# A hybrid encoder trunk on one core: the memory values' store moves eight pieces down SyncE's queue, the first w_in loads go ahead of the last memory products, and x's strips start in the memory stage's first half

## The chip, the cores and the metric

The kernel runs on one core of a Trainium2 chip. The metric is the device time of one execution in microseconds. It was run three times: 928.7, 930.54 and 930.84 us, median 930.54 us. A further execution was recorded by the hardware profiler and took 931.73 us; the profile and the trace are of that one.

## The reference

Two layers of one mixer. In each, the normed input is projected by one large matrix `w_in`, whose columns feed three groups of heads (a gated convolution, differential attention, and cross-attention into 256 memory tokens), and the three results are projected back by `w_out` and added to x. The memory side needs only `mem`, `mem_norm_g` and `w_mem_kv`:

```python
for l in range(DEPTH):                        # DEPTH = 2
    h = rmsnorm(x, norm_g[l])
    proj = h @ w_in[l]                        # (256, 2048) @ (2048, 7168)
    ...
    mn = rmsnorm(mem, mem_norm_g[l])
    mkv = mn @ w_mem_kv[l]                    # (256, 2048) @ (2048, 1024)
    mk = rmsnorm(mkv[..., :W_MEM].reshape(b, N_MEM, MEM_HEADS, MEM_HEAD_DIM), mem_k_norm_g[l])
    mv = mkv[..., W_MEM:].reshape(b, N_MEM, MEM_HEADS, MEM_HEAD_DIM)
    mq = rmsnorm(m_q.reshape(b, s, MEM_HEADS, MEM_HEAD_DIM), mem_q_norm_g[l])
    y_m = memory_attention(mq, mk, mv).reshape(b, s, W_MEM) * jax.nn.silu(m_g)

    y = jnp.concatenate([y_a, y_d, y_m], axis=-1) @ w_out[l]
    x = x + y
```

All inputs are float32. x and mem are 256 rows of 2048.

## The kernel before

**The products.** Every float32 operand is split into a rounded part `hi` and a remainder `lo`, and a product is three TensorE matmuls: hi by hi, hi by lo, lo by hi (`products`, L295 to L304). The stationary operand is a 128 by 128 piece of the turned activations (`memT` for the memory tokens, `xT` for x, `yT` for the mixer's results); the moving one is a 128 by 512 piece of a weight.

**Pieces of weights.** Weights stream through SBUF in pieces of 512 KB. A piece is loaded by SyncE's queue (SP in the profile) into one of four `raw` buffers; ScalarE (ACT) writes its `hi`, VectorE (DVE) its `lo`, into one of four buffers each; then TensorE uses it in twelve matmuls. A raw buffer is free for the next load when DVE has made `lo`, and a hi buffer when TensorE is done with the piece four places earlier.

**The memory stage.** The keys and values of the memory tokens are made for both layers at the start (L816 to L903). This document counts its pieces 0 to 31, sixteen for each layer: piece s is rows 128·k to 128·k + 127 of `w_mem_kv[l]`, with l, k = divmod(s, 16). `Memory.load` issues a load (L756, or L749 for a piece of w_in), `Memory.make` writes hi and lo (L773 and L774, or L766 for a piece of w_in), `Memory.times` the products. Two halves are accumulated beside each other, keys (half 0) and values (half 1), each in two PSUM banks of four. Pieces 14 and 15, 16 and 17, and 30 and 31 are taken in groups of two: within a group first the keys of both pieces, then the values. When the last keys of a layer are done, `keep_keys` copies them out of PSUM (ACT, L872, tile `kraw`); when the values are done, `keep_values` writes them to `mv` (ACT, L877), and for the second layer stores them to DRAM (SP, L880, tile `mvd`), from where they are loaded back in the second layer (L909).

**The first pieces of w_in.** After piece 31 come the eight pieces of w_in's first block, which are loaded, made and kept ready by the same class; this document calls them w0 to w7. w0 and w1 multiply the first quarter of `xT`, w2 and w3 the second, and so on. From then on `block` and `load_w` (L288 to L292) stream the rest of w_in and w_out in the same way.

**x's strips.** `xT` is made in four quarters q. `strips_by_rows` (L630 to L637) fetches a quarter of x by eight DMAs of 64 KB from GpSimd's queue (POOL) into an `xt` tile, of which there are two; for q = 0 a copy on POOL (L634) reads one value of a given tile first, which holds the DMAs back until that tile is written. After a number of pieces DVE turns the tile (L642, tile `xf`), and ACT and DVE write its hi and lo parts to `xT` (L261, L262). The tile of q = 2 is that of q = 0 again, and is free once DVE has turned it; so with q = 3 and q = 1. Behind the strips POOL's queue carries the DMAs that turn the memory keys (L724, L725).

**What sets the order.** Engines work off their queues in order. Calls wrapped in `pin` or `keep_in_program_order` keep their written order; the others are placed by a scheduler when the program is built. `beside(s)` hangs side work on piece s; `tasks` are generators that `run_side` resumes after a number of pieces (`later(g, n)`: n pieces from now). `m.load(ahead)` at L901 asks for loads up to four pieces ahead, after the products of a group are written.

Of the kernel before, what the change touches and what calls it, by code (L numbers as in the profile page):

```python
# [10 lines left out]
F32 = mybir.dt.float32  # L11
# [7 lines left out]
P = 128  # L19
D_MODEL = 2048  # L20
SEQ = 256
DEPTH = 2
NT = SEQ // P
KT = D_MODEL // P
W_MEM = 512
# [7 lines left out]
NB = 512  # L33
# [14 lines left out]
def encoder(ctx: ExitStack, tc: tile.TileContext, x, mem, norm_g, w_in, conv_w, conv_b,  # L48
            dq_g, dk_g, lq1, lk1, lq2, lk2, head_g, mem_norm_g, w_mem_kv, mq_g, mk_g, w_out, out):
    nc = tc.nc  # L50
    x, mem, out = x[0], mem[0], out[0]

    def pool(name, bufs, space=None):
        kw = {"space": space} if space is not None else {}
        return ctx.enter_context(tc.tile_pool(name=name, bufs=bufs, **kw))
# [7 lines left out]
    dram = pool("dram", 1, bass.MemoryType.DRAM)  # L63
# [6 lines left out]
    def nm(s):  # L70
        uid[0] += 1
        return f"{s}_{uid[0]}"
# [59 lines left out]
    def g_norm(l, k):  # L132
        return gx[:, l * KT + k:l * KT + k + 1]
# [56 lines left out]
    def rsqrt(t, n, vec=None):  # L190

        vec = vec or nc.vector
        y = small.tile([P, n], F32, tag=f"rs_y{n}", name=nm("rsy"))
        a = small.tile([P, n], F32, tag=f"rs_a{n}", name=nm("rsa"))
        yi = y.bitcast(I32)
        vec.tensor_scalar(yi, t.bitcast(I32), 1, None, ALU.logical_shift_right)
        vec.tensor_scalar(yi, yi, -1.0, float(0x5F3759DF), ALU.mult, ALU.add)
        for _ in range(3):
            vec.scalar_tensor_tensor(a, y, -0.5, y, ALU.mult, ALU.mult)
            vec.tensor_tensor(a, a, t, ALU.mult)  # L200
            vec.scalar_tensor_tensor(y, a, 1.5, y, ALU.add, ALU.mult)
        return y
# [4 lines left out]
    side, tasks = deque(), []  # L207
# [3 lines left out]
    def later(g, n):  # L211
        due[id(g)] = chunk[0] + n
        return g
# [40 lines left out]
    def split_T(dst, k, src, gain, pin=False):  # L254

        hi, lo = dst[:, 0, k, :], dst[:, 1, k, :]
        if gain is None:
            both = (nc.scalar.copy(hi, src),  # L258
                    nc.vector.tensor_tensor(lo, src, hi.bitcast(F32), ALU.subtract))
        else:  # L260
            both = (nc.scalar.activation(hi, src, AF.Copy, scale=gain),  # L261
                    nc.vector.scalar_tensor_tensor(lo, src, gain, hi.bitcast(F32), ALU.mult, ALU.subtract))  # L262
        if pin:
            for i in both:
                tc.keep_in_program_order(i)
        made.add((id(dst), k))
# [81 lines left out]
    R, HR, R2_64, R2_128, HR2, R2 = range(6)  # L348

    def col(st, which, t):  # L350
        return st[:, which, t:t + 1]
# [261 lines left out]
    def rows_T(src, k, n):  # L613

        pt = ps_t.tile([P, 2, SEQ], F32, tag="t", name=nm("pt"))
        for j in range(n):
            for t in range(NT):
                tc.keep_in_program_order(
                    nc.tensor.transpose(pt[:, j, t * P:(t + 1) * P], src(k + j, t), ident))  # L619
        return [pt[:, j, :] for j in range(n)]  # L620

    def strips_of(src):

        st = tmp.tile([P, SEQ // B, B * QT], F32, tag="e", name=nm("xt"))
        for b in range(NA):
            tc.keep_in_program_order(nc.sync.dma_start(
                st[b * B:(b + 1) * B], src[:, b * B * QT:(b + 1) * B * QT].rearrange("(n p) r -> p n r", p=B)))
        return st

    def strips_by_rows(src, after=None):  # L630

        st = tmp.tile([P, SEQ // B, B * QT], F32, tag="e", name=nm("xt"))
        if after is not None:
            tc.keep_in_program_order(nc.gpsimd.tensor_copy(st[:, 0, 0:1], after))  # L634
        for n in range(SEQ // B):
            tc.keep_in_program_order(nc.gpsimd.dma_start(  # L636
                st[:, n], src[n * B:(n + 1) * B].rearrange("p (b r) -> b p r", b=NA)))  # L637
        return st

    def turn_strips(st):  # L640
        whole = tmp.tile([P, QT, SEQ], F32, tag="sh", name=nm("xf"))
        tc.keep_in_program_order(nc.vector.transpose(whole.rearrange("p j (n i) -> p j n i", i=B),  # L642
                                                     st.rearrange("p n (c j) -> p j n c", j=QT)))
        return whole

    def x_turned(dst, l, q, src, after=None, wait=2):

        st = strips_of(src) if l else strips_by_rows(src, after)
        yield wait
        whole = turn_strips(st)  # L650
        yield
        for j in range(QT):
            split_T(dst, q * QT + j, whole[:, j], g_norm(l, q * QT + j), pin=True)
            if j % 2:
                yield
# [13 lines left out]
    def T_tile(what):  # L669
        kept.append(big.tile([P, 2, KT, SEQ], F32R, tag="T", name=nm(what)))  # L670
        return kept[-1]
# [11 lines left out]
    memT = T_tile("memT")  # L683
    ssm = const.tile([P, NT, 4], F32, name="ssm")

    pin = tc.keep_in_program_order

    def mem_tokens(lo, n):
        return pin(nc.sync.dma_start(xs[:, :, lo:lo + n], mem[:, lo:lo + n].rearrange("(t p) c -> p t c", p=P)))  # L689
# [4 lines left out]
    def mem_squares(c):  # L694

        for t in range(NT):
            sq = tmp.tile([P, NB], F32, tag="nat", name=nm("msq"), bufs=3)
            pin(nc.scalar.activation(sq, xs[:, t, c * NB:(c + 1) * NB], AF.Square, accum_out=ssm[:, t, c:c + 1]))

    def mem_stats():  # L700

        vec = Steps()
        t = small.tile([P, NT], F32, tag="ssum", name=nm("ssum"))
        y = stm[0]
        vec.tensor_reduce(t, ssm, AX.X, ALU.add)
        vec.tensor_scalar(t, t, 1.0 / D_MODEL, EPS, ALU.mult, ALU.add)
        r = rsqrt(t, NT, vec=vec)
        vec.tensor_copy(y[:, R], r)
        vec.scalar_tensor_tensor(y[:, R2_128], r, 1.0 / P, r, ALU.mult, ALU.mult)
        yield from vec.run(6)  # L710
# [97 lines left out]
    mkT, mv, stm, away = [], [], [], []  # L808
    m = Memory()
    xT = T_tile("xT")  # L810
# [24 lines left out]
    m.begin(1, 1, 0)  # L835
    m.begin(1, 0, 1)

    def beside(s):

        l, k = divmod(s, KT)  # L840
        if l == 0:
            if k % 2 and 3 <= k < KT - 1:
                m.split(k + 1, rows_T(mem_columns, k + 1, 2))
            if k in (3, 6):
                mem_tokens({3: 2, 6: 3}[k] * NB, NB)
            if k in (3, 5, 8, 11):
                mem_squares((3, 5, 8, 11).index(k))
            if k in (8, 10, 12):
                x_natural((k - 8) // 2)
            if k in (6, 7, 8):  # L850
                load_constants(k - 6)
            if k == 9:
                load_norm()
            if k == 11:
                tasks.append(later(mem_stats(), 1))
        else:
            if k == 0:
                x_natural(3)
            if k in (4, 5, 7, 8):
                for t in range(NT):  # L860
                    x_square((4, 5, 7, 8).index(k), t, pin=True)
            if k == 10:
                rest_of_constants()
            if k in (2, 3, 6, 9):
                q = k // 3
                tasks.append(later(x_turned(xT, 0, q, x[:, q * NB:(q + 1) * NB], stm[0][:, R, 0:1] if q == 0 else None,
                                            (3, 5, 5, 5)[q]), 0))

    def keep_keys(l):
        kraw = keep.tile([P, NT, NB], F32, tag="ga", name=nm("kraw"))  # L870
# [4 lines left out]
    def keep_values(l):  # L875
        for t in range(NT):
            pin(nc.scalar.activation(mv[l][:, t, :], m.acc[l, 1][t], AF.Copy, scale=col(stm[0], R, t)))  # L877
        if l > 0:
            away.append(dram.tile([P, NT, W_MEM], F32, name=nm("mvd")))
            nc.sync.dma_start(away[-1], mv[l])  # L880

    s = 1
    while s < DEPTH * KT:
        l, k = divmod(s, KT)
        group = (s, s + 1) if k in (KT - 2, 0) else (s,)
        for i in group:
            beside(i)
        for i in range(s, min(group[-1] + (2 if s == 1 else 3), DEPTH * KT + 1)):
            m.make(i)
        for half in range(2):  # L890
            for i in group:
                m.times(i, half)
            if s == 1 and half == 0:
                m.split(2, rows_T(mem_columns, 2, 2))
            if k == KT - 2:
                (keep_keys, keep_values)[half](l)
                if l + 1 == DEPTH and half == 0:
                    m.make(DEPTH * KT + 1)
        for i in group:
            for ahead in range(i + 1, i + 5):  # L900
                m.load(ahead)  # L901
            run_side(1)
        s = group[-1] + 1  # L903

    for l in range(DEPTH):
# [142 lines left out]
        if l + 1 < DEPTH:  # L1048
            xT = T_tile("xT")
# [50 lines left out]
```

## Time and profile before

| | us |
|---|---|
| median of three runs | 930.54 |
| the profiled execution's own time | 931.73 |
| its span, first to last instruction | 930.0 |
| TensorE busy in the span | 920.0 |
| VectorE busy | 668.6 |
| ScalarE busy | 495.2 |
| GpSimd busy | 37.7 |
| DMA engines, mean of what they moved | 231 GB/s |

Times in rows of the profile are counted from the first instruction. A row of the timeline gives start, length, engine, line and operation, with how many alike follow each other (x2), and in brackets how long the engine was idle before it and what ended that. A matmul's row shows its whole pipeline time of about 0.39 us; the next one starts 0.23 us after it. `PEclk` is the share of TensorE's clock that was granted.

### The profile page before, as it was taken

How to read it: one execution, taken by the hardware profiler on the slowest of the kernel's cores; microseconds unless marked ns; L12 is line 12 of the kernel's file. 1: busy time of each engine (PE TensorE's matmuls, PEld its weight loads, DVE VectorE, ACT ScalarE, POOL GpSimd, SP SyncE). 2: the span in 40 equal slices, each digit the busy share in tenths (PEclk: the TensorE clock that was granted, in tenths of full speed). 3: DMA queues.
4: the chain of work that ended last, by engine and by line, in shares of the span. 5: the costliest groups of instructions: out<-in, count | busy, mean ns of one | idle time of the engine just before them, and what ended most of it. 6: DMA issues, size and time to landing. Idle time of an engine off the chain costs nothing.

```text
span 930.0 us, 12261 instructions
## 1 busy us (share of the span) xinstructions
PE 920.0 (99%) x4168; PEld 762.2 (82%) x4168; DVE 668.6 (72%) x1176; ACT 495.2 (53%) x751; POOL 37.7 (4%) x66
## 2 busy tenths in 40 slices
PE   8999899999999999999999999999999999999998
PEld 6888688888888888888888888888888888888886
DVE  5579867857799787467667757887898777558652
ACT  5666645576465554445455544568554554446431
POOL 2155010000000000000000000000000000000000
PEclk9999899999999999999999999999999999999999
DMA  8889778885669999988587756886889889978662
GB/s 280 277 237 246 251 249 241 236 240 182 183 205 227 270 248 248 242 257 255 199 270 253 243 185 222 236 240 184 237 235 218 259 213 258 248 238 239 212 217 76
DMA packets 247022, 215.10 MB, mean 231 GB/s; under 512 B 132130, under 2 KB 172912, under 8 KB 246960
## 3 DMA queue, kind: packets, MB, share of 16 engines
q1 hardware_dynamic: 242080, 208.71, 76.6%
q0 software_dynamic: 3680, 4.56, 2.2%
q10 hardware_dynamic: 1200, 1.07, 0.4%
q8 instruction: 32, 0.52, 0.2%
q14 instruction: 30, 0.25, 0.1%
HBM read 193.26 MB, written 20.97 MB: 230 GB/s over the span
## 4 chain that ended last, share of the span: by engine, by line
PE 97%; DMA 1%; ACT 1%; SPq 0%; DVE 0%; issue 0%; DVEq 0%
PE acc L302 93%; PE po L442 2%; DMA raw<-in_w_mem_kv_dram 1%; PE s L595 1%; PE s L550 1%; PE s L549 1%; DMA raw<-in_w_in_dram 1%; PE pt L619 0%; ACT hi L766 0%; SPq L754 0%; SPq L689 0%; DVE lo L774 0%; ACT mv L877 0%; ACT hi L773 0%; ACT kraw L872 0%; ACT sq L359 0%
## 5 line engine op out<-in xcount | busy, mean ns | idle before, releaser
L302 PE MATMUL acc<-hi,xT 128*128 128x512 f32 x1792 | 563.8, 393 | 3.0 <-ACT hi L766 3.0
L291 ACT CAST hi<-raw 128x1024 fp32r<-128x1024 f32 x280 | 294.1, 1051 | 340.9 <-PE acc L302 286.5
L292 DVE TENSOR_TENSOR lo<-raw,hi 128x1024 fp32r<-128x1024 f32 x280 | 342.0, 1223 | 185.5 <-ACT hi L291 180.8
L302 PEld LDWEIGHTS acc<-hi,xT 128*128 128x128 f32 x1792 | 337.8, 189 | 72.7 <-ACT hi L766 3.4
L302 PE MATMUL acc<-lo,xT 128*128 128x512 f32 x896 | 350.4, 391 | 0.0
L302 PEld LDWEIGHTS acc<-lo,xT 128*128 128x128 f32 x896 | 169.0, 189 | 34.7 <-DVE lo L766 0.8
L302 PE MATMUL acc<-hi,yT 128*128 128x512 f32 x512 | 158.1, 389 | 0.0
L302 PEld LDWEIGHTS acc<-hi,yT 128*128 128x128 f32 x512 | 96.1, 188 | 20.1
L302 PE MATMUL acc<-lo,yT 128*128 128x512 f32 x256 | 99.7, 389 | 0.0
L302 PE MATMUL acc<-hi,memT 128*128 128x512 f32 x248 | 77.2, 395 | 0.4 <-ACT memT L258 0.4
L302 PEld LDWEIGHTS acc<-lo,yT 128*128 128x128 f32 x256 | 48.1, 188 | 9.8
L302 PEld LDWEIGHTS acc<-hi,memT 128*128 128x128 f32 x248 | 46.0, 188 | 10.4 <-ACT memT L258 0.8
L774 DVE SCALAR_TENSOR_TENSOR lo<-raw,cva,hi 128x1024 fp32r<-128x1024 f32 (+1 forms) x34 | 41.0, 1220 | 17.6 <-ACT hi L773 17.4
L302 PE MATMUL acc<-lo,memT 128*128 128x512 f32 x124 | 46.5, 392 | 0.8 <-DVE lo L774 0.8
L773 ACT ACTIVATE hi<-raw,cva 128x1024 fp32r<-128x1024 f32 (+1 forms) x34 | 36.5, 1096 | 13.6 <-DMA raw<-in_w_mem_kv_dram 6.7
L302 PEld LDWEIGHTS acc<-lo,memT 128*128 128x128 f32 x124 | 23.3, 188 | 6.3 <-DVE lo L774 1.5
L560 ACT ACTIVATE e<-e,mx 128x256 f32<-128x256 f32 x48 | 23.8, 498 | 1.4 <-DVE mx L556 1.4
L636 POOL DMA_DIRECT2D xt<-in_x_dram x32 | 21.5, 678 | 12.8 <-DMA xt<-in_x_dram 6.6
L261 ACT ACTIVATE xT<-xf,gx 128x256 fp32r<-128x256 f32 x32 | 14.3, 499 | 6.0 <-DVE xf L642 5.9
L404 DVE STREAM_TRANSPOSE sh<-sh 128x1024 f32<-128x1024 f32 (+2 forms) x14 | 17.3, 1237 | 0.0
L554 DVE SCALAR_TENSOR_TENSOR e<-dist,s 128x512 f32<-128x512 f32 x24 | 15.7, 680 | 2.2 <-PE s L550 1.7
L1061 DVE TENSOR_TENSOR xs<-acc,xs 128x256 f32<-128x256 f32 (+1 forms) x24 | 10.9, 504 | 7.8 <-PE acc L302 7.8
(161 smaller groups left out, 578.7 us busy)
## 6 DMA issues: line engine op xcount, KB each, us to landing
raw<-in_w_in_dram SPq DMA_DIRECT2D x192, 512.0 KB, 4.5
raw<-in_w_out_dram SPq DMA_DIRECT2D x64, 512.0 KB, 4.4
raw<-in_w_in_dram SPq DMA_DIRECT2D x64, 256.0 KB, 4.0
raw<-in_w_mem_kv_dram SPq DMA_DIRECT2D x30, 512.0 KB, 7.0
d<-sh SPq DMA_DIRECT2D x80, 128.0 KB, 3.9
sh<-d SPq DMA_DIRECT2D x64, 128.0 KB, 4.4
d<-yn SPq DMA_DIRECT2D x40, 64.0 KB, 4.0
yn<-d SPq DMA_DIRECT2D x40, 64.0 KB, 3.7
```

The costliest lines, as they stand in the source:

```text
L261: both = (nc.scalar.activation(hi, src, AF.Copy, scale=gain), nc.vector.scalar_tensor_tensor(lo, src, gain, hi.bitcast(F32), ALU.mult, ALU ...
L291: nc.scalar.copy(hi, raw)
L292: nc.vector.tensor_tensor(lo_, raw, hi.bitcast(F32), ALU.subtract)
L302: i = nc.tensor.matmul(acc, left, right, start=start, stop=stop)
L404: tc.keep_in_program_order(nc.vector.transpose(src, src))
L442: nc.tensor.matmul(po[:, t, :], eT[:, i, t, k, :], v[:, k, h * P:(h + 1) * P], start=k == 0, stop=k == NT - 1)
L554: nc.vector.scalar_tensor_tensor(e[:, c], dist, -slopes[h], s[c], ALU.mult, ALU.add)
L560: nc.scalar.activation(e[:, c, i], e[:, c, i], AF.Exp, bias=mx[:, c, i:i + 1], accum_out=sm[:, c, i:i + 1])
L636: tc.keep_in_program_order(nc.gpsimd.dma_start(st[:, n], src[n * B:(n + 1) * B].rearrange("p (b r) -> b p r", b=NA)))
L773: both = (nc.scalar.activation(hi[:, j], raw[:, j], AF.Copy, scale=g), nc.vector.scalar_tensor_tensor(lo[:, j], raw[:, j], g, hi[:, j].bit ...
L774: nc.vector.scalar_tensor_tensor(lo[:, j], raw[:, j], g, hi[:, j].bitcast(F32), ALU.mult, ALU.subtract))
L1061: nc.vector.tensor_tensor(xc, acc[t][:, lo:lo + n], xc, ALU.add)
```

## The change

Three edits, all in the memory stage. The store of the second layer's values becomes a task that is issued eight pieces later, pinned to its place in SP's queue. For the last group (pieces 30 and 31) the loads of the pieces up to w3 are asked for before the group's products rather than after them. x's strips are asked for at pieces 13 and 15 of the first half and 3 and 6 of the second, rather than at 2, 3, 6 and 9 of the second; the first quarter's copy on POOL now reads column 13 of `memT` in place of the norm's `stm`; and the number of pieces between fetching and turning becomes 5, 7, 7 and 8 rather than 3, 5, 5 and 5.

```diff
@@ -835,6 +835,9 @@
+    def x_strips(q, after, wait):
+        tasks.append(later(x_turned(xT, 0, q, x[:, q * NB:(q + 1) * NB], after, wait), 0))
+
     def beside(s):
...
@@ -853,6 +856,8 @@
             if k == 11:
                 tasks.append(later(mem_stats(), 1))
+            if k in (13, 15):
+                x_strips(k // 14, memT[:, 0, 13, 0:1].bitcast(F32) if k == 13 else None, 2 * (k // 14) + 5)
         else:
...
@@ -861,10 +866,8 @@
             if k == 10:
                 rest_of_constants()
-            if k in (2, 3, 6, 9):
-                q = k // 3
-                tasks.append(later(x_turned(xT, 0, q, x[:, q * NB:(q + 1) * NB], stm[0][:, R, 0:1] if q == 0 else None,
-                                            (3, 5, 5, 5)[q]), 0))
+            if k in (3, 6):
+                x_strips(k // 3 + 1, None, k // 3 + 6)
...
@@ -876,8 +879,12 @@
         if l > 0:
-            away.append(dram.tile([P, NT, W_MEM], F32, name=nm("mvd")))
-            nc.sync.dma_start(away[-1], mv[l])
+            tasks.append(later(put_away(mv[l]), 8))
+
+    def put_away(values):
+        away.append(dram.tile([P, NT, W_MEM], F32, name=nm("mvd")))
+        pin(nc.sync.dma_start(away[-1], values))
+        yield
...
@@ -887,6 +894,9 @@
         for i in range(s, min(group[-1] + (2 if s == 1 else 3), DEPTH * KT + 1)):
             m.make(i)
+        if group[-1] == DEPTH * KT - 1:
+            for ahead in range(s + 2, s + 6):
+                m.load(ahead)
         for half in range(2):
...
@@ -897,8 +907,9 @@
         for i in group:
-            for ahead in range(i + 1, i + 5):
-                m.load(ahead)
+            if group[-1] < DEPTH * KT - 1:
+                for ahead in range(i + 1, i + 5):
+                    m.load(ahead)
             run_side(1)
```

What this does to the queues is shown at three places, in the order in which the built programs hold the instructions.

SP's queue where the memory stage ends; `raw` rows at L756 are pieces of w_mem_kv, at L749 pieces w0 to w7 of w_in, `mvd` is the store of the values. Before:

```order
L756 DMA raw_894<-in_w_mem_kv_dram 128x1024
L756 DMA raw_916<-in_w_mem_kv_dram 128x1024
L749 DMA raw_942<-in_w_in_dram 128x2x512
L749 DMA raw_964<-in_w_in_dram 128x2x512
L880 DMA mvd_1007<-mv_113 128x1024
L749 DMA raw_1009<-in_w_in_dram 128x2x512
L749 DMA raw_1013<-in_w_in_dram 128x2x512
L749 DMA raw_1131<-in_w_in_dram 128x2x512
L749 DMA raw_1153<-in_w_in_dram 128x2x512
```

And now:

```order
L756 DMA raw_898<-in_w_mem_kv_dram 128x1024
L756 DMA raw_918<-in_w_mem_kv_dram 128x1024
L749 DMA raw_946<-in_w_in_dram 128x2x512
L749 DMA raw_968<-in_w_in_dram 128x2x512
L749 DMA raw_974<-in_w_in_dram 128x2x512
L749 DMA raw_976<-in_w_in_dram 128x2x512
L749 DMA raw_1129<-in_w_in_dram 128x2x512
L749 DMA raw_1151<-in_w_in_dram 128x2x512
L886 DMA mvd_1169<-mv_113 128x1024
```

The store stood between w1 and w2; it now stands behind w5.

POOL's queue at the strips of x, a copy and eight DMAs of 64 KB for each of the four quarters, and the first DMAs for the keys (`kd`). Before:

```order
L114 DMA gx<-in_norm_g_dram 128x8x4
L634 COPY xt_660<-stm 128x1
L636 DMA xt_660<-in_x_dram 128x1x128 x8
L636 DMA xt_691<-in_x_dram 128x1x128 x8
L636 DMA xt_772<-in_x_dram 128x1x128 x8
L636 DMA xt_853<-in_x_dram 128x1x128 x8
L724 DMA kd_918<-sh_588 32x4x256 x4
```

And now:

```order
L114 DMA gx<-in_norm_g_dram 128x8x4
L634 COPY xt_540<-memT_107 128x1
L636 DMA xt_540<-in_x_dram 128x1x128 x8
L636 DMA xt_589<-in_x_dram 128x1x128 x8
L636 DMA xt_706<-in_x_dram 128x1x128 x8
L636 DMA xt_791<-in_x_dram 128x1x128 x8
L724 DMA kd_920<-sh_607 32x4x256 x4
```

The queue's order is the same; what its first copy waits for is another tile.

ACT's queue at the border between the two layers, pieces 15 to 18 (L773) and the copies of the first layer's keys and values out of PSUM. Before:

```order
L773 ACTIVATE hi_519<-raw_474,cva 128x1024
L773 ACTIVATE hi_540<-raw_502,cva 128x1024
L773 ACTIVATE hi_544<-raw_535,cva 128x1024
L773 ACTIVATE hi_593<-raw_577,cva 128x1024
L872 COPY kraw_560<-acc_155 128x512
L872 COPY kraw_560<-acc_156 128x512
L877 ACTIVATE mv_111<-acc_174,stm 128x512
```

And now:

```order
L773 ACTIVATE hi_519<-raw_474,cva 128x1024
L773 ACTIVATE hi_550<-raw_502,cva 128x1024
L773 ACTIVATE hi_554<-raw_535,cva 128x1024
L773 ACTIVATE hi_612<-raw_587,cva 128x1024
L875 COPY kraw_570<-acc_155 128x512
L875 COPY kraw_570<-acc_156 128x512
L880 ACTIVATE mv_111<-acc_174,stm 128x512
```

Nothing moved here but the numbers of buffers and lines: in both programs the keys' copies stand behind the conversion of piece 18.

## The prediction

> **What bounds the kernel now.** First the page's shares of the span and its list of idle times, to see which engine sets the time; then TensorE's own timeline, to see where it is not working.
>
> ```profile
> PE 920.0 (99%) x4168; PEld 762.2 (82%) x4168; DVE 668.6 (72%) x1176; ACT 495.2 (53%) x751; POOL 37.7 (4%) x66
> L302 PE MATMUL acc<-hi,xT 128*128 128x512 f32 x1792 | 563.8, 393 | 3.0 <-ACT hi L766 3.0
> ```
>
> TensorE is busy for 99% of the span, and the largest group of matmuls lost 3.0 us, all of it to one wait for a `hi` written at L766. The table of stretches shows how clean the rest is:
>
> ```profile
> 13.80:104.40 90.60, 90.60 (x408) 74.24 (x408) 69.53 (x134) 61.06 (x105) 33.69 (x54) 1.00 0.87 250
> 107.40:113.60 6.20, 6.16 (x14) 4.38 (x15) 6.17 (x10) 4.46 (x5) 0.00 (x0) 0.50 0.75 243
> 113.60:925.90 812.30, 812.30 (x3708) 677.26 (x3706) 585.47 (x1018) 421.64 (x631) 2.73 (x5) 1.00 0.79 228
> ```
>
> The columns are length, then busy time and count of PE, PEld, DVE, ACT and POOL, the granted clock, the DMA share and GB/s. From 13.8 to 104.4 and from 113.6 to 925.9 TensorE has no idle time at all and the full clock. A change to the memory stage can therefore win at most what is lost between 104.4 and 113.6, and any new wait of TensorE adds to the time one for one.
>
> What is lost there is read from TensorE's timeline:
>
> ```profile
> 104.02 0.39 PE L302 MATMUL acc<-hi,xT 128*128 128x512 f32 x1
> 107.36 1.22 PE L302 MATMUL acc<-hi,xT 128*128 128x512 f32 x2 [2.95 <-ACT hi L766]
> ...
> 113.76 0.40 PE L302 MATMUL acc<-lo,xT 128*128 128x512 f32 x1
> ```
>
> and why, from the chain of waits of that place, in order of time:
>
> ```profile
> 100.52 0.34 SPq L880
> ...
> 100.97 5.27 DMA raw<-in_w_in_dram
> 106.24 0.02 issue
> 106.26 1.05 ACT hi L766
> ```
>
> SP's queue had nothing else to do; it stood before the store of the values, which needs `mv`, which needs the last product of the memory stage:
>
> ```profile
> SPq L880 <- ACT mv L877: 11.0, 1, 11.0
> ```
>
> w2's load stands behind that store, goes out at 100.97, lands after 5.27 us, is converted in 1.05 us, and TensorE, done with w1 at 104.4, starts w2 at 107.36. Then it runs at half clock until 113.6.
>
> **The change part by part.**
>
> *The store behind w5, the loads ahead of the products.* This removes the wait. With a raw buffer free, w2's load no longer waits for the values. It takes the raw buffer of piece 30, and w3 that of piece 31, so what gates them now is DVE's `lo` of these pieces:
>
> ```profile
> 91.68 1.28 DVE L774 SCALAR_TENSOR_TENSOR lo<-raw,cva,hi 128x1024 fp32r<-128x1024 f32 x1
> 94.07 1.27 DVE L774 SCALAR_TENSOR_TENSOR lo<-raw,cva,hi 128x1024 fp32r<-128x1024 f32 x1
> ```
>
> So w2 can be issued at 92.96 and w3 at 95.34, against 100.97 and 101.44. Even with the longest time to landing that a load of weights shows in this stage (9.4 us, below), w2 is there at 102.4; its `hi` goes into the buffer of piece 30, free when the memory products end at 98.8, so ACT makes it by 103.5, 0.7 us before TensorE wants it at 104.25; DVE's `lo`, 1.2 us behind, comes at 104.7, when the third matmul of w2 wants it. w4 and w5 wait for the `lo` of w0 and w1 and also go out ahead of the store. Behind the store wait w6 and w7 and then the stream of w_in; it stands where `mv` is long written, and costs its issue alone, 0.34 us on a queue with 11 us to spare. Nobody reads `mvd` before the second layer.
>
> The gain: a full-speed piece is 24 matmuls in 5.47 us in the first rows of the chain, 0.228 us each.
>
> ```profile
> 17.14 5.47 PE acc L302 x24
> ```
>
> From the matmul at 104.02 to the one at 113.76 stand 15 starts (14 of them in the half-clock row above). At full pace that is 15 x 0.228 = 3.42 us; it took 9.74. Lost: 6.3 us, about 3.1 of it idle and 3.2 by the clock. All of it goes if TensorE no longer waits: **-6.3**.
>
> *x's strips earlier.* No instruction is added; 32 DMAs of 64 KB, four turns of 2.0 us and the writes of `xT` move. On POOL the copy waited 24 us for `stm`:
>
> ```profile
> 52.47 1.24 POOL L634 COPY xt<-stm 128x1 f32<-128x1 f32 x1 [23.98 <-DVE stm L186]
> 54.00 5.41 POOL L636 DMA_DIRECT2D xt<-in_x_dram  x8 [0.29 <-POOL xt L634]
> 41.72 0.37 ACT L258 CAST memT<-pt 128x256 fp32r<-128x256 f32 x1 [0.49 <-DVE memT L259]
> ```
>
> Column 13 of `memT` is written by ACT's row at 41.72, so the copy runs at 42.1, and the first eight strips are issued from 43.6 to 49.0, 10.4 us earlier, the next eight behind them as their semaphores come free. DVE turns the first quarter two pieces earlier than now, about 62.9; strips land at most 10.4 us after issue (next fence), by 59.4, so DVE does not wait. The two tiles then free POOL for the third and fourth quarter by 7 to 10 us sooner, and the keys' DMAs behind them too. All this is slack.
>
> What is not slack is the DMA engines between 44 and 56, which the strips had left alone. SP's loads of pieces 17, 18 and 19 are alone there, and the ones behind them are not:
>
> ```profile
> L756 SPq DMA_DIRECT2D raw<-in_w_mem_kv_dram x1: 328/328/328, 45.7 to 45.7; - x1
> DMA to landing us min/median/max: 3.1/3.1/3.1
> ...
> L756 SPq DMA_DIRECT2D raw<-in_w_mem_kv_dram x1: 328/328/328, 48.0 to 48.0; - x1
> DMA to landing us min/median/max: 4.8/4.8/4.8
> ...
> L756 SPq DMA_DIRECT2D raw<-in_w_mem_kv_dram x11: 327/328/328, 53.7 to 80.3; - x11
> DMA to landing us min/median/max: 6.1/8.3/9.4
> ...
> L636 POOL DMA_DIRECT2D xt<-in_x_dram x8: 675/675/731, 54.0 to 58.7; - x8
> DMA to landing us min/median/max: 6.6/9.0/10.4
> ```
>
> With strips beside it a load takes 6.1 to 9.4 us instead of 3.1 to 4.8. For pieces 17 and 19 that is covered by buffers. Piece 18 is the tight one:
>
> ```profile
> 52.93 1.16 ACT L773 ACTIVATE hi<-raw,cva 128x1024 fp32r<-128x1024 f32 x1
> 53.98 1.05 ACT L872 COPY kraw<-acc 128x512 f32<-128x512 f32 x2
> ...
> 54.55 0.63 PE L302 MATMUL acc<-hi,memT 128*128 128x512 f32 x2
> ```
>
> Its load lands at 48.0 + 4.8 = 52.8, ACT converts it at 52.93, and only behind that copies the first layer's keys out of PSUM, the first bank by about 54.5. The second matmul of the row at 54.55, at 54.79, is the first of the second layer, and it writes the very bank that the copy has just emptied. There is no slack: whatever the load of piece 18 is late, `kraw` is late and TensorE waits. The queue order of ACT is the same in the changed program, so this stays. What the added delay is no row of before can show, since no strip flies there. Bounds: below 0 (the load still lands after 4.8 us; a gain is excluded, since TensorE does not wait there now), above 9.4 - 4.8 = 4.6. I take the quickest of the loads among strips, 6.1 - 4.8 = **+1.3**, because only a load and a half stand in SP's queue at that time, where the slower rows have three, and because the strips have just begun.
>
> [...]
>
> ```profile
> 47.00:48.00 1.00, 1.00 (x6) 0.79 (x5) 1.00 (x2) 0.14 (x1) 0.00 (x0) 1.00 0.98 356
> 51.00:52.00 1.00, 1.00 (x6) 0.85 (x5) 1.00 (x1) 1.00 (x2) 0.00 (x0) 1.00 0.04 16
> ```
>
> The second row shows why piece 18's load took 4.8 us alone: the engines are nearly idle at 51 to 52, so one straggler of the sixteen finished it. That it happens again is assumed; without it the load has 1.7 us of room and the wait is gone.
>
> *Does the new wait cost the clock too?* The clock fell after a wait of 2.95 us and did not after these two:
>
> ```profile
> 12.74 0.51 PE L302 MATMUL acc<-hi,memT 128*128 128x512 f32 x1 [0.36 <-ACT memT L258]
> 13.80 0.50 PE L302 MATMUL acc<-lo,memT 128*128 128x512 f32 x1 [0.56 <-DVE lo L774]
> ```
>
> Bounds 0 and 3.2 us, the loss found above. 1.3 lies nearer to 0.56 than to 2.95: **0**. [...]
>
> **The sum.** Span 930.0 - 6.3 + 1.3 + 0 = 925.0, and the profiled execution's own time 931.73 - 5.0 = 926.7. The median of the runs, 930.54, lies 1.2 below that execution; less the same, **925.5**.
>
> **The rivals.**
>
> *No new wait* (25%). Piece 18's load meets few strips, or the straggler does not come. For it: it is issued at 48.0, when the first strips only begin to land (43.6 + 6.6 = 50.2). Against it: they move before they land. 930.54 - 6.3 = 924.2.
>
> *The new wait takes the clock as well* (14%). For it: the only wait of the trace between 0.6 and 3 us did. 925.5 + 3.2 = 928.7, within 0.3% of before.
>
> *The wait changes place* (8%), and this one ends slower. Piece 18's load lands as late as the latest of those among strips, 9.4 us after issue: 4.6 us of wait, more than the 2.95 that took the clock, so 4.6 + 3.2 = 7.8 against 6.3 won: 932.0. It decides from a delay of about 3.1 us on (3.1 + 3.2 = 6.3). For it: the median of those rows is 8.3. Against it: they had three loads before them.
>
> *The change doesn't do what it says* (6%): w2 is late for another reason, and TensorE stands at 104 as before. For it: w2's `hi` needs ACT between the copies of keys and values. Against it: the room that is left even at the slowest landing. About 930.5, with the forecast's wait 931.8 at worst.
>
> **How the numbers follow.** The forecast has 47%; its own range is 924.6 (wait 0.4) to 927.3 (wait 3.1 without the clock). A measurement of this kernel tells about 0.3%, 2.8 us, from no change, so faster means below 927.75. The forecast and the first rival are faster, 72%, less 2 for a base that was as low as 928.7 in one run: 0.70. The clock rival, the undone change and part of the slower one lie within 2.8 us of 930.54: 0.25. Slower by more: 0.05. The range for 8 in 10 goes from 923.6 (the first rival, less 0.6 for the spread of the runs) to 929.0 (the clock rival) and leaves out the last two.
>
> **What would show it.** Right: SP's `mvd` waits for nothing and stands behind six loads of w_in; TensorE has no idle time around 104 and clock 1.00 throughout; at about 55 us a wait of some 1.3 us of the first matmul of the second layer, ended by ACT's `kraw`, with piece 18's load landing about 6 us after issue. Wrong: that load lands after 5 us or less (924.2), or a stretch at clock 0.50 follows 55 us (928.7), or a wait appears where DVE stands before a turn of a strip, which I take to be covered.

## The result, and the profile after

| | before | after |
|---|---|---|
| median, us (7 runs of each, taken together) | 930.84 | 927.93 |
| range, us | 928.7 to 931.87 | 926.49 to 929.68 |
| the profiled execution's own time, us | 931.73 | 929.68 |
| its span, us | 930.0 | 927.9 |

The ratio is 0.997, with a 95% interval of 0.9957 to 0.9984: the change is faster by 2.9 us, or 1.5 to 4.0 us. The forecast had 925.5 us and a range of 923.6 to 929.0. The sign was right, and the gain is a little over half of the one forecast. The median lies inside the range, but above the band that the forecast gave itself (924.6 to 927.3), and 0.2 us above the 927.75 that it had set as the limit of faster; the interval of the ratio still lies wholly below 1.

The stall at 104 us is gone. The first rows are of the page and of SyncE's timeline, the last two of the table of stretches (columns as before: length, busy time of PE, PEld, DVE, ACT, POOL, granted clock, DMA share, GB/s).

```profile
L302 PE MATMUL acc<-hi,xT 128*128 128x512 f32 x1792 | 561.2, 391 | 0.0
```

```profile
87.07 16.77 SPq L749 DMA_DIRECT2D raw<-in_w_in_dram  x6
105.37 0.34 SPq L886 DMA_DIRECT2D mvd<-mv  x1
107.12 2.23 SPq L749 DMA_DIRECT2D raw<-in_w_in_dram  x2
```

```profile
61.50:923.90 862.40, 862.40 (x3928) 718.67 (x3926) 633.06 (x1118) 458.28 (x691) 16.26 (x26) 1.00 0.79 230
104.00:106.00 2.00, 2.00 (x10) 1.65 (x10) 2.00 (x3) 2.00 (x4) 0.00 (x0) 1.00 0.74 216
```

The large group of matmuls has lost its 3.0 us of idle time. SP issues six loads of w_in in a row; the store follows them at 105.37, after 1.53 us in which it stands for `mv`, which ACT has written at 105.34. It delays nothing: w6's load behind it goes out at 107.12, when DVE is done with a `lo` (107.10). From 61.5 to 923.9 us, where its last matmuls are, TensorE is never idle and has the full clock.

A new stall stands at 55 us. It is the only idle time of TensorE after the first 6 us. TensorE's timeline, then the chain of waits of that place (start, length, what):

```profile
54.72 0.39 PE L302 MATMUL acc<-hi,memT 128*128 128x512 f32 x1
57.48 0.50 PE L302 MATMUL acc<-hi,memT 128*128 128x512 f32 x1 [2.37 <-ACT kraw L875]
```

```profile
48.25 0.03 DVE rsy L186
48.28 7.42 DMA raw<-in_w_mem_kv_dram
55.70 0.02 issue
...
55.81 0.09 ACT hi L773
55.90 0.96 issue
56.86 0.57 ACT kraw L875
57.44 0.04 issue
57.48 29.08 PE acc L302 x120
```

This is the mechanism of the forecast step by step: the load of piece 18 is issued at 48.28 and takes 7.42 us instead of 4.82, ACT converts the piece at 55.81 and only then copies the first layer's keys out of PSUM, and the first product of the second layer waits for the bank. The forecast had 1.3 us; it is 2.37. The view of transfers for SP's loads of 47 to 60 us and POOL's strips of 40 to 60 us shows what flies beside piece 18:

```profile
L756 SPq DMA_DIRECT2D raw<-in_w_mem_kv_dram x5: 327/328/328, 48.3 to 58.3; - x5
DMA to landing us min/median/max: 7.4/8.3/9.5
```

```profile
L636 POOL DMA_DIRECT2D xt<-in_x_dram x16: 675/675/733, 42.9 to 53.9; - x16
DMA to landing us min/median/max: 3.2/6.2/8.0
```

All sixteen strips of the first two quarters are issued from 42.9 to 53.9, the second quarter right behind the first; there is no pause in which piece 18 could land alone.

In this execution the wait took the clock as well. The table of stretches:

```profile
55.00:57.00 2.00, 0.11 (x1) 0.00 (x0) 0.15 (x2) 1.19 (x2) 0.00 (x0) 1.00 0.95 229
57.00:59.00 2.00, 1.52 (x5) 1.25 (x6) 1.27 (x1) 2.00 (x5) 0.00 (x0) 0.77 1.05 334
59.00:61.00 2.00, 2.00 (x7) 1.53 (x6) 0.92 (x2) 0.82 (x3) 0.00 (x0) 0.50 1.04 275
61.00:63.00 2.00, 2.00 (x9) 1.67 (x8) 1.04 (x1) 1.45 (x2) 0.00 (x0) 0.88 1.04 399
```

The granted clock is 0.77, 0.50 and 0.88 in three stretches of 2 us. What is missing from 1.00 adds up to (0.23 + 0.50 + 0.12) x 2 = 1.7 us: one period of 3.41 us at half clock, from 58.08 to 61.50 us. The mean clock of the runs tells how often that happens: it is 0.998 in two of the seven (929.68 and 929.18 us) and 0.999 or 1.000 in the other five (926.49 to 928.04). So the loss belongs to some executions, and the median of 927.93 has the wait without it.

The profiled spans then add up: 930.0 - 6.3 (old stall) + 2.4 (new wait) + 1.7 (clock) = 927.8, and 927.9 was measured.

### The profile page after: what moved, and what is told of

Same layout as the page of the kernel before. It is cut to its first block, busy times and chain, and to the rows that moved or that the text cites. A ratio compares the mean times of both kernels' runs of the same rounds, so it can differ in the third digit from the quotient of the medians.

```text
span 927.9 us, 12263 instructions
## 1 busy us (share of the span) xinstructions
PE 919.7 (99%) x4168; PEld 763.6 (82%) x4168; DVE 668.2 (72%) x1176; ACT 495.1 (53%) x751; POOL 36.5 (4%) x66
## 4 chain that ended last, share of the span: by engine, by line
PE 97%; DMA 2%; DVE 1%; ACT 1%; issue 0%; SPq 0%; DVEq 0%; ACTq 0%
PE acc L302 92%; PE po L442 2%; DMA raw<-in_w_mem_kv_dram 2%; PE s L595 1%; PE s L550 1%; PE s L549 1%; PE acc L791 1%; DVE lo L774 0%; ACT hi L773 0%; PE pt L619 0%; ACT msq L698 0%; ACT kraw L875 0%; DVE memT L259 0%; SPq L689 0%; DVE xs L1072 0%
## 5 line engine op out<-in xcount | busy, mean ns | idle before, releaser
L773 ACT ACTIVATE hi<-raw,cva 128x1024 fp32r<-128x1024 f32 (+1 forms) x34 | 36.2, 1095 | 11.9 <-DMA raw<-in_w_mem_kv_dram 8.8
```

The costliest lines, as they stand in the source:

```text
L773: both = (nc.scalar.activation(hi[:, j], raw[:, j], AF.Copy, scale=g), nc.vector.scalar_tensor_tensor(lo[:, j], raw[:, j], g, hi[:, j].bit ...
```

## The experiments

Three theories of the new stall. **A**: the strips' transfers beside piece 18's load make it late, and ACT's order (convert piece 18, then copy the keys) hands that on to TensorE. **B**: it is the order of the work: the moved turns and DMAs of the strips make ACT or DVE late at 55. **C**: it is the first edit, the store and the loads of w_in. Each kernel was run beside the kernel before on the same chip; the edits are shown against the changed kernel.

**One edit at a time.** The first kernel has the store and the loads of w_in as changed, and the strips as before:

```diff
-            if k in (13, 15):
-                x_strips(k // 14, memT[:, 0, 13, 0:1].bitcast(F32) if k == 13 else None, 2 * (k // 14) + 5)
...
-            if k in (3, 6):
-                x_strips(k // 3 + 1, None, k // 3 + 6)
+            if k in (2, 3, 6, 9):
+                q = k // 3
+                tasks.append(later(x_turned(xT, 0, q, x[:, q * NB:(q + 1) * NB], stm[0][:, R, 0:1] if q == 0 else None,
+                                            (3, 5, 5, 5)[q]), 0))
```

> The store's delay and the early loads of w_in, with x's strips as in the kernel before. Theory A (the strips' transfers make piece 18's load late, and ACT's queue hands that on to the keys' copy and TensorE): no wait at 55 us, none at 104, clock 1.00 throughout; the 6.3 us are won whole, 930.84 - 6.3 = 924.5, ratio 0.993. Rival C (the loads and the store in their new places cause the wait at 55): the wait of about 2.4 us stays, about 927.5, ratio 0.997.

Measured: 925.62 us (924.53 to 926.04, five runs), ratio 0.9944 [0.9932, 0.9956]. The chain of waits at 48 us and TensorE's timeline at 110:

```profile
47.94 5.04 DMA raw<-in_w_mem_kv_dram
...
53.08 0.95 ACT hi L773
54.03 0.11 issue
54.14 1.05 ACT kraw L872 x2
```

```profile
110.69 0.50 PE L302 MATMUL acc<-lo,xT 128*128 128x512 f32 x1 [0.23 <-DVE lo L766]
```

With the strips where they were, piece 18's load takes 5.04 us and TensorE has no wait at 55, as A expected. There is no stall at 104. What is left is 0.23 us at 110, where DVE had stood 1.66 us before a turn of the memory keys, whose DMAs stand on POOL behind the later strips.

The second kernel has the other edit alone:

```diff
-            tasks.append(later(put_away(mv[l]), 8))
+            away.append(dram.tile([P, NT, W_MEM], F32, name=nm("mvd")))
+            nc.sync.dma_start(away[-1], mv[l])
...
-        if group[-1] == DEPTH * KT - 1:
-            for ahead in range(s + 2, s + 6):
-                m.load(ahead)
...
-            if group[-1] < DEPTH * KT - 1:
-                for ahead in range(i + 1, i + 5):
-                    m.load(ahead)
+            for ahead in range(i + 1, i + 5):
+                m.load(ahead)
```

> x's strips begun in the first half, with the store and the loads of w_in as in the kernel before. Theory A: the wait of about 2.4 us at 55 and the old one of about 3 us at 104 with its half clock: 930.84 + 2.4 to 4.1 (with or without a window of half clock at 57) = 933.2 to 934.9, ratio 1.003 to 1.004. Rival C: no wait at 55, 930.8, ratio 1.000. If the early strips help the end of the memory stage, the wait at 104 is shorter than 2.95 us.

Measured: 933.06 us (930.09 to 936.39, twelve runs), ratio 1.0025 [1.0012, 1.0038]: slower than before. The chain of waits, then TensorE's timeline:

```profile
48.71 8.76 DMA raw<-in_w_mem_kv_dram
...
58.63 0.57 ACT kraw L875
59.20 0.04 issue
59.24 0.79 PE acc L302
```

```profile
59.24 0.79 PE L302 MATMUL acc<-hi,memT 128*128 128x512 f32 x1 [3.72 <-ACT kraw L875]
112.54 0.73 PE L302 MATMUL acc<-hi,xT 128*128 128x512 f32 x2 [2.24 <-ACT hi L766]
113.80 0.79 PE L302 MATMUL acc<-lo,xT 128*128 128x512 f32 x1 [0.53 <-DVE lo L766]
```

The load takes 8.76 us here and the wait is 3.72. The stall behind the store is there again, only later: `mvd` goes out at 105.97, and w2's load, issued behind it at 106.42, lands at 111.42. The two waits there, 2.24 and 0.53 us, are together a little shorter than the 2.95 of before. So the strips bring the stall at 55 without the other edit, and C falls. The time is just under the 933.2 to 934.9 that A expected.

**The copy of the keys ahead of piece 18.** This kernel leaves every transfer where the change put it and turns round two instructions on ACT: piece 18 is converted behind the keys' copy rather than ahead of it.

```diff
-                if s < KT + 2:
+                if s < KT + 3:
...
+                if l == 0 and half == 0:
+                    m.make(KT + 2)
```

> The changed kernel, with piece 18 converted behind the copy of the first layer's keys instead of ahead of it. Theory A: piece 18's load still lands 7 us or more after its issue, but the keys' copy does not stand behind it, and TensorE has no idle time at 55: 924.5, ratio 0.993. Rival B (the strips edit delays TensorE there in another way, by the order of DVE or of TensorE itself): the wait of 2.4 us stays, 927.9, ratio 0.997.

Measured: 925.35 us (924.52 to 925.89, five runs), ratio 0.9942 [0.9929, 0.9956]. ACT's timeline:

```profile
53.39 1.07 ACT L875 COPY kraw<-acc 128x512 f32<-128x512 f32 x2 [0.61 <-PE acc L302]
55.62 1.15 ACT L773 ACTIVATE hi<-raw,cva 128x1024 fp32r<-128x1024 f32 x1 [1.16 <-DMA raw<-in_w_mem_kv_dram]
```

Piece 18 is as late as in the changed kernel, converted at 55.62 against 55.81, but ACT began to copy the keys out of PSUM at 53.39, and TensorE does not wait: it has no idle time from 5.1 us to its last matmul. The late load alone costs nothing; it needs ACT's order to reach TensorE. That is the second link of A; the first, that the strips make the load late, is tested by holding them back, below.

**The edit of one kernel with the order of the other.** The first experiment's strips as before, with the keys' copy first:

> The kernel of the store and loads alone, with piece 18 converted behind the keys' copy as well. Theory A: nothing left to win there, 924.5, ratio 0.993, the same as with the strips early and the same as with the store alone. If the early strips are worth something of their own once the keys' copy is free, the kernel with them is faster than this one by more than 0.1%.

Measured: 925.60 us (925.08 to 926.06, five runs), ratio 0.9945 [0.9934, 0.9957]. This answers what the early strips are worth once nothing is paid for them. TensorE's timeline has one row with a wait:

```profile
110.40 0.50 PE L302 MATMUL acc<-lo,xT 128*128 128x512 f32 x1 [0.52 <-DVE lo L766]
```

The early strips take away this half microsecond (0.23 in the first experiment). The medians, 925.35 with them and 925.60 without, don't tell the two apart.

**The early strips held back.** All strips as in the changed kernel, but the first quarter's copy on POOL waits for `stm` as it did before the change:

```diff
-                x_strips(k // 14, memT[:, 0, 13, 0:1].bitcast(F32) if k == 13 else None, 2 * (k // 14) + 5)
+                x_strips(k // 14, stm[0][:, R, 0:1] if k == 13 else None, 2 * (k // 14) + 5)
```

> The changed kernel, with one thing undone: the copy on POOL that holds back the first quarter's strips reads the norm's stm again, as before the change. All strips are then issued from about 52.5 us on; their number and the places where DVE turns them stay as in the changed kernel. Theory A (strips that fly beside piece 18's load make it late): that load lands about 4.8 to 5.1 us after issue, TensorE has no wait at 55. But the turn of the second quarter now stands on DVE before strips that are issued at 58 to 68 and land near 78, so a wait of about 1 us may appear around 75 to 80; median 925.3 to 926.5. Theory B (the changed places of the turns and of the strips' DMAs on POOL and DVE make ACT late at 55): the wait of 2.4 us at 55 stays; 927.5 to 928.5.

Measured: 929.16 us (927.87 to 930.13, twelve runs), ratio 0.9978 [0.997, 0.9987]. Piece 18's load, issued at 47.54, landed at 52.42, after 4.88 us, and there is no wait at 55, although DVE's turns and the strips keep their changed order: B falls, and A holds. The time alone would have misled: it is some 3 us above what A expected and nearer to B's 927.5 to 928.5, but the loss is elsewhere. A second stall was expected, of about 1 us and at the second quarter's turn. It came at the first, and larger. DVE's timeline and TensorE's:

```profile
63.71 1.28 DVE L774 SCALAR_TENSOR_TENSOR lo<-raw,cva,hi 128x1024 fp32r<-128x1024 f32 x1 [1.24 <-ACT hi L773]
70.49 1.98 DVE L642 STREAM_TRANSPOSE xf<-xt 128x1024 f32<-128x1024 f32 x1 [5.49 <-DMA xt<-in_x_dram]
72.39 0.13 DVE L186 SCALAR_TENSOR_TENSOR rsa<-rsy 128x8 f32<-128x8 f32 x1
72.44 1.28 DVE L774 SCALAR_TENSOR_TENSOR lo<-raw,cva,hi 128x1024 fp32r<-128x1024 f32 x1
```

```profile
73.77 0.79 PE L302 MATMUL acc<-lo,memT 128*128 128x512 f32 x1 [2.70 <-DVE lo L774]
82.18 0.50 PE L302 MATMUL acc<-lo,memT 128*128 128x512 f32 x1 [0.45 <-DVE lo L774]
```

The last strip of the first quarter landed at 70.17; DVE stood 5.49 us before its turn, the `lo` of a piece stood behind that, and TensorE waited 2.70 us. It is the same pattern once more: an engine in order, in front of it a transfer that is not there, behind it something that TensorE needs. The early turns only work with the early strips.

**Eight strips instead of sixteen.** The first quarter early, the second from piece 2 of the second half:

```diff
-            if k in (13, 15):
-                x_strips(k // 14, memT[:, 0, 13, 0:1].bitcast(F32) if k == 13 else None, 2 * (k // 14) + 5)
+            if k == 13:
+                x_strips(0, memT[:, 0, 13, 0:1].bitcast(F32), 5)
...
+            if k == 2:
+                x_strips(1, stm[0][:, R, 0:1], 5)
```

> The changed kernel, with only the first quarter's eight strips asked for in the first half; the second quarter is asked for at piece 2 of the second half and held back by stm, so its strips go out from about 52 us on, when piece 18's load has been flying for 4 us. Tells how much of that load's 7.4 us is due to the first eight strips, and how much to the second eight. If the lateness goes with the number of strips in flight: load 5.5 to 6.5 us, a wait of TensorE at 55 of 0.5 to 1.5 us, no loss of clock, median 926 to 927 (this is the case that the prediction had priced at 1.3 us). If the first eight alone make it: load 7 us or more, wait about 2.4 us, 927.5 to 928. If only the second eight make it: load 4.8 to 5.1 us, no wait, 925.3 to 925.8.

Measured: 926.13 us (925.35 to 929.4, six runs), ratio 0.9953 [0.9936, 0.9969]. The chain of waits, then TensorE's timeline:

```profile
47.97 6.23 DMA raw<-in_w_mem_kv_dram
54.20 0.02 issue
...
55.37 0.57 ACT kraw L877
```

```profile
55.98 0.50 PE L302 MATMUL acc<-hi,memT 128*128 128x512 f32 x1 [1.19 <-ACT kraw L877]
```

The load takes 6.23 us and the wait is 1.19. The second quarter's strips go out at 53.97, just before the load lands at 54.20. Load, wait and median are as expected for the case in which the lateness goes with the number of strips. With no strips beside it the load took 4.82 to 5.13 us, with eight early strips 6.23, with sixteen 7.42 to 8.76: the more strips, the later, by one trace of each kernel. What makes 8.76 out of 7.42 in the kernel with the strips alone is not shown.

In the profiled executions the losses of TensorE and the span go together (us; waits in the first 14 us, each under 1.3 us, are left out):

| kernel | load of piece 18, us | idle at 55 | idle later | half clock, lost | span |
|---|---|---|---|---|---|
| before | 4.82 | 0 | 2.95 | 3.4 | 930.0 |
| changed | 7.42 | 2.37 | 0 | 1.7 | 927.9 |
| store and loads alone | 5.04 | 0 | 0.23 | 0 | 924.3 |
| strips alone | 8.76 | 3.72 | 2.77 | 3.4 | 934.2 |
| changed, keys first | 7.65 | 0 | 0 | 0 | 923.6 |
| store and loads, keys first | 5.13 | 0 | 0.52 | 0 | 924.0 |
| changed, strips held | 4.88 | 0 | 3.15 | 1.7 | 928.4 |
| changed, one quarter | 6.23 | 1.19 | 0 | 0 | 924.8 |

Span less the three losses is between 923.5 and 924.3 in every row, so these losses are all that tells the kernels apart, to 0.8 us.

**The best version** is the changed kernel with the keys' copy first: 925.35 us, faster than before (0.9942) and, by 2.6 us of the medians, than the change. Its lead over the two kernels at 925.6 is within the spread. So what early strips add once the keys are copied first is not shown to be more than nothing. An extra buffer for raw pieces, which might let piece 18's load go out earlier, was not tried.

## Why the prediction came out as it did

**The old stall, -6.3: right.** It was made against the profiled execution, and there it holds: 931.73 - 6.3 = 925.4, and the kernels without any stall of note run at 925.35 to 925.62. The loads go out as worked out, w2's at 94.4 us and w3's at 96.6, when DVE's `lo` of pieces 30 and 31 is there (94.42 and 96.61), and the cover on ACT and DVE was enough. The store stands behind w5 as forecast, but not where `mv` is long written: it waited 1.53 us for it, with no load behind it that TensorE had to wait for. The rival by which the change doesn't do what it says fell. The expectations of three experiments took the same 6.3 off the median (930.84 - 6.3 = 924.5) and came out 0.9 to 1.1 us too low; the next step is why.

**The step from the profile to the median, -1.2: wrong.** The prediction took 1.2 us off because the profiled execution lay that far above the median of the runs, as if that were a constant of the execution. The runs point to the old stall instead. The seventeen runs of before beside the first four experiments spread over 4.2 us (928.44 to 932.67); the fifteen runs of the three kernels without a stall of note spread over 1.5 us (924.52 to 926.06). The profiled execution of before had two periods of half clock; by the mean clock (0.996 to 0.999) other executions had fewer. Between medians the first experiment won 5.2 us (930.84 to 925.62) and not 6.3, and in the three kernels without a stall of note the profiled execution lies only 0 to 0.4 us above the median. So what the profiled execution of before lay above the median was, most of it, a part of the loss being removed, and it was taken off twice. Without this step the sum is 926.7.

**The new wait, +1.3: the mechanism was right, the size was not.** Place, order and release are as written. The step that failed is "I take the quickest of the loads among strips, 6.1 - 4.8 = +1.3", with its two reasons, "only a load and a half stand in SP's queue at that time" and "the strips have just begun". The wait measured 2.37 us, inside the bounds of 0 to 4.6. The prediction's own text had the second quarter's strips following the first as their semaphores come free, and did not count them: with eight strips the load took 6.23 us and the wait was 1.19 us, the number that was forecast; with sixteen it was 7.42.

**The clock, 0: right for most runs.** It was argued for a wait of 1.3 us. With the larger wait that came (2.37 us in the profiled execution; the other runs' waits are not on record), five of seven runs lost nothing and two lost about 1.7 us by their mean clock. The profiled execution is one of the two, and shows the stretch at 0.50 that the prediction had named as a sign of being wrong. The rival that added 3.2 us had the size of two periods; one was what came.

**The assumption that the straggler comes again: right.** The load needs 4.88 to 5.13 us in the three kernels without strips beside it, and in the first of them the engines' share between 51 and 52 us is 0.05 at 16 GB/s, where it was 0.04 at 16 GB/s before, both less than one engine of the sixteen (0.0625). So the rival "no new wait" had no room. Its 924.2 lies 1.4 us under the 925.62 of the kernel without early strips: it too takes 6.3 off the median.

**The wait that changes place and ends slower** did not come for the change. The kernel with the strips alone has a load near the 9.4 us priced (8.76) and a wait of 3.72 us with one period of half clock, 5.4 us together; that is still less than the 6.3 won. Its 933.06 us are slower than before because the old stall is there as well.

Together: 926.7 for the old stall alone without the step to the median, and 1.1 more for the larger wait, makes 927.8; the median is 927.93.

## What to carry to other kernels

Before moving transfers into a quiet stretch, list the loads that are alone there and follow each landing through the engines that work in order: what counts is not whether the load is covered, but what stands behind its consumer on that engine. Where a conversion waits for a transfer and an eviction of PSUM stands behind it, put the eviction first; here those two instructions were worth 2.6 us, nearly as much as the change. And when a profiled execution lies above the median, ask whether the stall to be removed is what put it there, before taking the difference off again.

## What the hardware showed that was not expected

**Half clock came in whole periods of 3.41 us.** In every trace that has one, the stretch at half clock behind a wait is 3.41 us or twice that, and how many periods a wait costs varies from run to run: 2.95 us of idle time took two in the profiled execution of before, 3.72 us took one, 2.70 us took one in the profiled execution and by the mean clock (0.997 against 0.999 or 1.000) none in the eleven other runs of that kernel, 1.19 us took none in the profiled execution, while one of the five others of that kernel (929.4 us, its wait not on record) has a mean clock of 0.998. The changes of the clock also lie on one grid in three traces: with the strips alone it is full from 10.99 to 58.78 us, half to 62.19, full to 113.39 and half to 116.81, which is 14, 1, 15 and 1 times 3.413 us; before, it is full from 4.36 to 106.76 us and half to 113.59, 30 and 2 times the same; in the changed kernel full from 10.30 to 58.08 and half to 61.50, 14 and 1 times. What decides how many periods a wait costs, no run here shows. A single price for a wait of 2 to 3 us is therefore an average over 0, 1.7 and 3.4 us.

**Strips hold up a load for longer than their bytes explain.** In the kernel with eight early strips four had landed by 47.64, before piece 18's load was issued, and four landed while it flew. In the changed kernel the same four landed during the load; of the second quarter, whose first strip was issued 0.02 us ahead of the load, none landed before it, but much of their bytes moved beside it. The rows of the DMA queues for the load's flight show this. They give packets, MB, and the time of the packets as a share of the time of sixteen engines; q1 carries SP's loads, q0 the strips. First the kernel before (48.00 to 52.82), then the changed kernel (48.28 to 55.70), then q0 of the kernel with eight early strips (47.97 to 54.20):

```profile
q1 hardware_dynamic: 178, 0.60, 37.5%
q1 hardware_dynamic: 250, 0.89, 51.1%
q0 software_dynamic: 752, 0.65, 50.3%
q0 software_dynamic: 320, 0.27, 22.2%
```

At the 356 GB/s of the 47 to 48 us row in the prediction, the strips' 0.65 MB move in 1.8 us and the 0.27 MB in 0.8 us. The load came 2.3 to 2.6 us (7.42) and 1.1 to 1.4 us (6.23) later than alone (4.82 to 5.13). Two things for the rest are on record, and no run separates them. Beside each other the bytes of both queues move more slowly: alone, SP's took 3.0 us of all sixteen engines for each MB (37.5% of 4.82 us for 0.60 MB); in the changed kernel SP's took 4.3 and the strips' 5.7. And piece 17, which stands ahead of piece 18 in SP's queue, was late as well: it landed 4.7 us after its issue rather than 3.1, and 4.1 with eight early strips.
